# A hybrid encoder layer on one core: the first group's weights in another layout, and part of them on another queue

## The chip, the cores and the metric

The kernel runs on one core of a Trainium2 chip. The time is the device time of one execution in microseconds, the median of several runs. The engines are TensorE (PE, with its weight loads as PEld), VectorE (DVE), ScalarE (ACT), GpSimd (POOL) and SyncE (SP); SyncE and ScalarE both issue DMAs, each on a queue of its own.

## What is computed

A layer of 1024 positions and width 1024 in float32. One wide product, two mixers, a gated merge, an output product and a layer norm:

```
h = x @ w_in + b_in                      # 1024 x 6144: xa za xb zb ga gb
ya = RG-LRU(causal_conv4(xa)) * silu(za)
yb = MultiScalePool(xb) * silu(zb)
y  = (sigmoid(ga) * (ya @ w_proj_a) + sigmoid(gb) * (yb @ w_proj_b)) @ w_out + b_out
out = LayerNorm(alpha * x + y)
```

The change concerns the start of the first product alone: the blocks of `ga` that are computed first.

## The kernel before, in words

Every float32 matrix is split into a high part (a cast to fp32r on ScalarE, `CAST`) and a low part (raw minus high, on VectorE, `TENSOR_TENSOR`), and each product is three matmul passes: high by high, weight high by data low, weight low by data high (`passes`, lines 454 to 457). The input product is done in groups of two weight blocks of 128 columns. Later groups use sums of quarters so as to need seven products for eight; the first one is plain.

That first group takes the blocks 32 and 36 of `w_in` (block 0 and block 1 below; `first` in line 959). In DRAM a block lies as 128 partitions x 8 chunks x 128 columns. The contraction has eight chunks of 128, split in two halves (called `h` in the weights' views, `kh` elsewhere) of four chunks `k`. Tiles `w0r0`, `w0r1` take the raw blocks, `w0h` and `w0l` their high and low parts (lines 959 to 961). `dma_w0(n, a, b, h)` loads of block n the chunks a to b of the halves h (line 971), and `split_w0` makes its high and low part (line 975). A chunk of one half is a row of 128 columns, 512 B; two chunks side by side are 1 KB.

The data come as `xq`, in four chunks q with two rows each, loaded into `xr` by `dma_x` (line 978), split by `split_x` into `x13h`/`x13l` (two quarters), `xb` and `x`. A row of 1024 columns holds two quarters of 512 positions. TensorE's order for chunk 0 is fixed (lines 1082 to 1092): quarter (0, 0) with block 0, in two pieces of 256 columns; quarter (1, 1) with block 0, which needs the second half of block 0's first weights and the second half of row 0 (`dma_x(0, 0, HALF[1])`); quarters (0, 0) and (1, 1) with block 1, which need block 1's first weights (`dma_w0(1, 0, 1)`); then quarter (0, 1), which reads `xb`. Its second matmul reads the low part. Six matmuls of zeros (`ps_warm`) run before all that.

The order of the instructions is not that of the text. A planner (`Plan.order`, lines 252 to 379) runs all tasks through a modelled time and emits them in the order in which it starts them. TensorE and GpSimd keep the written order. On the others, of the tasks that are ready the one with the smallest due time goes first, then the one written first. The due time of a task is the smaller of what its readers leave it (their due time less its own modelled time) and TensorE's modelled clock where it is written plus `late`, which is 40 us, and within `nc.within(-2 * SOON)` it is -4 us (line 266). The modelled clock is 2.88 us where the first loads are written. A load on SyncE is costed at 270 GB/s and 0.07 us of issue, on ScalarE at 270 GB/s and 0.45 us. A task may be held back for one that is about to be ready and due earlier (lines 358 to 361). `sum57(q)` (line 1042) is a VectorE subtraction of 128x1024 for the sums of quarters; it needs row 0 and the first half of row 1, and is due later than the low parts around it.

The loads are written in this order: the first half of block 0's first weights (ScalarE's queue), the two pieces of row 0's first half (SyncE, within -4 us), the second half of block 0's first weights (ScalarE's), block 1's first weights (ScalarE's), row 0's second half, row 1 in two halves, and the rest on SyncE. Later loads wait for a free completion semaphore of an earlier one.

Of the kernel before, what the change touches and what calls it, by code (L numbers as in the profile page):

```python
# [11 lines left out]
F32 = mybir.dt.float32  # L12
F32R = mybir.dt.float32r
AF = mybir.ActivationFunctionType
ALU = mybir.AluOpType

P = 128
S = 1024
D = 1024
NK = D // P  # L20
# [380 lines left out]
def layer_kernel(ctx: ExitStack, tc: tile.TileContext, xq, x, w_in, par, wg, w_pool, wpa, wpb, w_out, rows, out):  # L401
    nc = Plan(tc)
# [18 lines left out]
    def wt(name, dt=F32R, shape=(P, 2, H)):  # L421
        return wpool.tile(list(shape), dt, tag="w", name=name)
# [7 lines left out]
    def et(name):  # L430
        return epool.tile([P, H], F32, tag="e", name=name)
# [9 lines left out]
    V, A = nc.vector, nc.scalar  # L441
# [8 lines left out]
    def split(raw, hi, lo):  # L450
        A.copy(hi, raw)
        V.tensor_tensor(lo, raw, hi.bitcast(F32), ALU.subtract)
# [147 lines left out]
    def blocks_of(kind, c):  # L600
        if kind == "A":
            return XA + c, ZA + c
        if kind == "B":
            return XB + c, ZB + c
        sec = GA if c < 4 else GB
        return sec + c % 4, sec + c % 4 + 4
# [297 lines left out]
    def b_pool(g):  # L904
# [15 lines left out]
        if g == 1:  # L920
# [5 lines left out]
    sp, m, nl, y, z, z2, acc = (const.tile([P, 8], F32, name=n)  # L926
                                for n in ("sp", "sp_m", "sp_nl", "sp_y", "sp_z", "sp_z2", "sp_acc"))
# [29 lines left out]
    for i in range(WARM):  # L957
        nc.tensor.matmul(psw, warm[:, 0:P], warm, start=True, stop=True)
    first = blocks_of(*order[0])
    wr, wh, wl = [[f(f"{t}{n}") for n in range(2)] for t, f in  # L960
                  (("w0r", lambda n: wt(n, F32)), ("w0h", wt), ("w0l", wt))]
# [6 lines left out]
    def w0_part(t, n, a, b):  # L968
        return t[n].rearrange("p h (k m) -> p h k m", m=P)[:, :, a:b, :]

    def dma_w0(n, a, b, h=slice(0, 2)):

        (A if a == 0 else nc.sync).dma_start(w0_part(wr, n, a, b)[:, h], w_in[first[n]].rearrange("p (h k) m -> p h k m", h=2)[:, h, a:b, :])

    def split_w0(n, a, b, h=slice(0, 2)):
        split(*(w0_part(t, n, a, b)[:, h] for t in (wr, wh, wl)))

    def dma_x(q, i, sl=slice(0, S)):
        nc.sync.dma_start(xr[q][i][:, sl], xq[q, i][:, sl])
# [21 lines left out]

    PARTS = [slice(0, H // 2), slice(H // 2, H)]
    dma_w0(0, 0, 1, slice(0, 1))
    with nc.within(-2 * SOON):
        for sl in PARTS:
            dma_x(0, 0, sl)
    dma_w0(0, 0, 1, slice(1, 2))
    dma_w0(1, 0, 1)
    dma_x(0, 0, HALF[1])
    dma_x(0, 1, HALF[0])  # L1010
    dma_x(0, 1, HALF[1])
# [65 lines left out]
    def each(f, qs, *a):  # L1077
        for q in qs:
            f(q, *a)

    split_w0(0, 0, 1, slice(0, 1))
    for kh, h in ((0, 0), (1, 1), (0, 1), (1, 0)):
        if kh == h == 1:
            split_w0(0, 0, 1, slice(1, 2))
        for sl in PARTS if kh == h == 0 else (slice(0, H),):
            split_x(0, kh, h, sl)
            mm0(0, kh, h, 0, sl)
        if kh == h == 1:
            split_w0(1, 0, 1)
            mm0(0, 0, 0, 1)  # L1090
        if kh or h:
            mm0(0, kh, h, 1)
# [264 lines left out]
    for i, (n, j) in enumerate(steps):  # L1357
# [7 lines left out]
        if j == 1:  # L1365
            a, c, m1, um = [[None] * KQ for _ in range(4)]
        X_, W_ = ([(hi_[:, k, :], lo_[:, k, :]) for hi_, lo_ in ops[i][o:o + 2] for k in range(2)] for o in (0, 2))
        for g in range(KQ):
# [17 lines left out]
            if (n, j) in DONE:  # L1386
                d, h = DONE[n, j]
                d += g
                if j == 3:
                    t, u = ps, et(f"c12_{n}{g}") if n == "b" else None  # L1390
                else:
                    t = u = m1[g] if j == 2 else um[g][:, HALF[h]]
# [12 lines left out]
            if (n, j, g) in CASTS:  # L1405
                k = CASTS.index((n, j, g))
# [89 lines left out]
    a, c = ([None] * KQ for _ in range(2))  # L1496
# [89 lines left out]
```

## Time and profile before

| | us |
|---|---|
| median of three runs (742.25 to 745.42) | 742.84 |
| the profiled execution | 743.09 |
| its span, first to last instruction | 741.3 |
| TensorE busy | 732.1 |
| VectorE busy | 599.6 |
| ScalarE busy | 459.0 |

The rows come from that one profiled execution; times count from the start of its span. A line of the timeline gives start, length, engine, line (L388 for all, since one line emits every task), operation, output<-inputs, and in brackets how long the engine sat idle before it and who ended that. Matmul lengths include their pipelined end, so the distance between starts tells the pace. Buffer numbers are left out of names, so `w0h` stands for either block.

### The profile page before, as it was taken

The numbers are of one execution on the slowest core, as the hardware profiler recorded it, in microseconds if no ns is written. First come the engines' busy times: TensorE is split into PE (matmuls) and PEld (weight loads), VectorE is DVE, ScalarE is ACT, GpSimd is POOL, SyncE is SP. The second block draws the span as 40 slices with busy tenths as digits, with TensorE's granted clock in tenths as the row PEclk, the third lists the DMA queues.
The fourth block names the chain that finished last, engine by engine and source line by source line (L and its number), as shares of the span: only waits on it lengthen the run. The fifth ranks groups of instructions, "written<-read, shape, count | busy, mean of one in ns | idle before, by whom it ended". The sixth has DMA issues, their size and how long they took to land.

```text
span 741.3 us, 8792 instructions
## 1 busy us (share of the span) xinstructions
PE 732.1 (99%) x3249; PEld 599.0 (81%) x3249; DVE 599.6 (81%) x749; ACT 459.0 (62%) x587; POOL 68.2 (9%) x118
## 2 busy tenths in 40 slices
PE   8999999999999999999999999999999999999996
PEld 6887887888788878888888888888888888888885
DVE  7999796959696878977986767879948886999676
ACT  7686959686877868688844445446543555324473
POOL 0071011111101111100011000100000000000021
PEclk9999999999999999999999999999999999999999
DMA  8237988588988989842187944998679996758657
GB/s 328 96 137 194 273 190 259 139 243 217 307 166 214 321 214 281 213 115 99 45 200 155 213 113 157 277 336 319 229 248 298 317 330 230 261 206 233 179 88 139
DMA packets 64227, 158.98 MB, mean 214 GB/s; under 512 B 4340, under 2 KB 8308, under 8 KB 64120
## 3 DMA queue, kind: packets, MB, share of 16 engines
q1 hardware_dynamic: 43512, 106.26, 41.3%
q0 software_dynamic: 20112, 51.91, 33.6%
q8 instruction: 25, 0.41, 0.2%
q10 hardware_dynamic: 560, 0.26, 0.1%
q14 instruction: 18, 0.15, 0.1%
HBM read 137.43 MB, written 77.07 MB: 289 GB/s over the span
## 4 chain that ended last, share of the span: by engine, by line
PE 98%; DMA 1%; DVE 1%; DVEq 0%; issue 0%
PE a_A L388 11%; PE a_B L388 11%; PE a_G L388 11%; PE oa L388 6%; PE pa_a L388 6%; PE pa_b L388 6%; PE c_B L388 6%; PE c_A L388 6%; PE c_G L388 5%; PE ps_pool L388 3%; PE oc L388 3%; PE pc_b L388 3%; PE pc_a L388 3%; PE e_B L388 3%; PE e_A L388 3%; PE ps_s L388 3%
## 5 line engine op out<-in xcount | busy, mean ns | idle before, releaser
L388 ACT ACT_TABLE_LOAD x38 | 48.8, 1283 | 3.0 <-issue 2.3
L388 DVE TENSOR_TENSOR i<-i,xc 128x1024 f32<-128x1024 f32 x8 | 9.8, 1224 | 26.6 <-ACT i L388 26.6
L388 DVE SCALAR_TENSOR_TENSOR xc<-xp,par_sb,xc 128x1024 f32<-128x1024 f32 x24 | 30.7, 1279 | 0.3
L388 PE MATMUL pa_a<-oh,oh 128*128 128x512 f32 x64 | 24.9, 389 | 0.0
L388 PE MATMUL pa_a<-oh,ol 128*128 128x512 f32 x64 | 24.9, 389 | 0.0
L388 PE MATMUL pa_b<-oh,oh 128*128 128x512 f32 x64 | 24.9, 389 | 0.0
L388 PE MATMUL pa_b<-ol,oh 128*128 128x512 f32 x64 | 24.9, 389 | 0.0
L388 PE MATMUL pa_b<-oh,ol 128*128 128x512 f32 x64 | 24.9, 389 | 0.0
L388 PE MATMUL pa_a<-ol,oh 128*128 128x512 f32 x64 | 24.9, 389 | 0.0
L388 ACT ACTIVATE zb<-zb,par_sb 128x1024 f32<-128x1024 f32 (+1 forms) x16 | 15.0, 939 | 13.7 <-DVE zb L388 13.6
L388 ACT ACTIVATE r<-ps_g,par_sb 64x512 f32<-64x512 f32 x32 | 21.9, 684 | 2.1 <-PE ps_g L388 1.2
L388 ACT ACTIVATE i<-ps_g,par_sb 64x512 f32<-64x512 f32 x32 | 21.9, 685 | 1.9 <-DVE r L388 1.4
L388 PE MATMUL c_A<-x64h,wd_A 128*128 128x512 f32 x64 | 21.0, 389 | 0.0
L388 PE MATMUL c_B<-x64h,wd_B 128*128 128x512 f32 x64 | 21.0, 389 | 0.0
L388 PE MATMUL ps_pool<-mixh,wp 128*128 128x512 f32 x64 | 20.6, 393 | 0.0
L388 POOL DMA_DIRECT2D out<-y x7 | 8.5, 1210 | 132.1 <-ACT sd L388 118.7
L388 PE MATMUL e_A<-x,wah_A 128*128 128x512 f32 x64 | 19.7, 389 | 0.0
L388 PE MATMUL e_B<-x,wah_B 128*128 128x512 f32 x64 | 19.7, 389 | 0.0
L388 POOL COPY paced<-pace 128x1 f32<-128x1 f32 x17 | 6.6, 387 | 128.7 <-ACT pace L388 128.7
L388 PE MATMUL c_G<-x64h,wd_G 128*128 128x512 f32 x56 | 18.4, 389 | 0.0
L388 DVE TENSOR_TENSOR_SCAN r<-a,i 128x1024 f32<-128x1024 f32 x8 | 18.3, 2282 | 0.1
L388 PE MATMUL e_G<-x,wah_G 128*128 128x512 f32 x56 | 17.2, 389 | 0.0
(521 smaller groups left out, 2535.9 us busy)
## 6 DMA issues: line engine op xcount, KB each, us to landing
sg<-sg SPq DMA_DIRECT2D x16, 512.0 KB, 3.6
ra_A<-in_w_in SPq DMA_DIRECT2D x8, 512.0 KB, 7.2
rb_A<-in_w_in SPq DMA_DIRECT2D x8, 512.0 KB, 7.8
xb<-bias SPq DMA_DIRECT2D x4, 1024.0 KB, 15.9
ya<-r SPq DMA_DIRECT2D x8, 512.0 KB, 6.3
xb<-in_x POOLq DMA_DIRECT2D x4, 1024.0 KB, 9.3
ra_B<-in_w_in SPq DMA_DIRECT2D x8, 512.0 KB, 4.8
rb_B<-in_w_in SPq DMA_DIRECT2D x8, 512.0 KB, 6.2
```

The source lines that it names most:

```text
L388: getattr(getattr(nc, t.op[0]), t.op[1])(*a, **k)
```

## The change

Block 0 and block 1 are stored in DRAM chunk by chunk with the two halves side by side (chunk k of half 0, chunk k of half 1), the same on the chip in the raw tile. A load of one chunk with both halves is then one row of 1 KB for each partition, where it was two of 512 B, and one of two chunks is a row of 2 KB, where it was two of 1 KB. The split reads the raw tile through a view that puts the halves back in place. ScalarE's queue is used for chunk 0 of block 0 only; block 1's first weights go on SyncE's queue. The second half of block 0's first weights and block 1's first weights are now written within the block of the small due times. The high part of block 0's first half is made by VectorE (`V.tensor_copy`) where ScalarE made it.

```diff
+    def w0_raw(n, a, b):
+        t = wr[n].rearrange("p a b -> p (a b)").rearrange("p (k h m) -> p h k m", h=2, m=P)
+        return t[:, :, a:b, :]
+
     def dma_w0(n, a, b, h=slice(0, 2)):
 
-        (A if a == 0 else nc.sync).dma_start(w0_part(wr, n, a, b)[:, h], w_in[first[n]].rearrange("p (h k) m -> p h k m", h=2)[:, h, a:b, :])
-
-    def split_w0(n, a, b, h=slice(0, 2)):
-        split(*(w0_part(t, n, a, b)[:, h] for t in (wr, wh, wl)))
+        lo_, hi_ = 2 * P * a + P * h.start, 2 * P * (b - 1) + P * h.stop
+        (A if n == a == 0 else nc.sync).dma_start(wr[n].rearrange("p a b -> p (a b)")[:, lo_:hi_],
+                                                  w_in[first[n]].rearrange("p k m -> p (k m)")[:, lo_:hi_])
+
+    def split_w0(n, a, b, h=slice(0, 2), high=A.copy):
+        raw, u, v = w0_raw(n, a, b)[:, h], w0_part(wh, n, a, b)[:, h], w0_part(wl, n, a, b)[:, h]
+        high(u, raw)
+        V.tensor_tensor(v, raw, u.bitcast(F32), ALU.subtract)
...
     with nc.within(-2 * SOON):
         for sl in PARTS:
             dma_x(0, 0, sl)
-    dma_w0(0, 0, 1, slice(1, 2))
-    dma_w0(1, 0, 1)
+        dma_w0(0, 0, 1, slice(1, 2))
+        dma_w0(1, 0, 1)
...
-    split_w0(0, 0, 1, slice(0, 1))
+    split_w0(0, 0, 1, slice(0, 1), V.tensor_copy)
...
+    w0 = blocks(w_in[0])
+    for n in (32, 36):
+        w0[n] = w0[n].reshape(P, 2, 4, P).transpose(0, 2, 1, 3).reshape(P, NK, P)
...
-        "w_in": blocks(w_in[0]),
+        "w_in": w0,
```

## Rows read from the trace of the kernel before

**Rows 1.** The page, busy time of each engine (us, share of span, instructions).
```profile
PE 732.1 (99%) x3249; PEld 599.0 (81%) x3249; DVE 599.6 (81%) x749; ACT 459.0 (62%) x587; POOL 68.2 (9%) x118
```

**Rows 2.** Waits of TensorE from 10 us on: total, times, longest.
```profile
PE ps_s L388 <- DVE xb L388: 0.3, 1, 0.3
```

**Rows 3.** Chain that ended last, in order of time: start, length, what.
```profile
0.72 3.21 DMA w0r<-in_w_in
...
29.08 2.72 PE a_A L388 x12
```

**Rows 4.** Timeline of TensorE, 4 to 14 us.
```profile
4.42 0.58 PE L388 MATMUL ps_s<-x13h,w0h 128*128 128x256 f32 x1
...
5.49 0.41 PE L388 MATMUL ps_s<-x13l,w0h 128*128 128x256 f32 x1
5.71 0.41 PE L388 MATMUL ps_s<-x13h,w0l 128*128 128x256 f32 x1
...
6.47 0.79 PE L388 MATMUL ps_s<-x13l,w0h 128*128 128x512 f32 x1
...
7.75 0.50 PE L388 MATMUL ps_s<-x13h,w0h 128*128 128x512 f32 x1
...
9.27 0.39 PE L388 MATMUL ps_s<-xb,w0h 128*128 128x512 f32 x1
9.95 0.50 PE L388 MATMUL ps_s<-xb,w0h 128*128 128x512 f32 x1 [0.30 <-DVE xb L388]
10.29 0.40 PE L388 MATMUL ps_s<-xb,w0l 128*128 128x512 f32 x1
```

**Rows 5.** Timeline of ScalarE, 0 to 12 us.
```profile
3.77 0.41 ACT L388 CAST x13h<-xr 128x256 fp32r<-128x256 f32 x1 [0.17 <-DMA xr<-in_xq]
...
4.61 0.29 ACT L388 CAST w0h<-w0r 128x128 fp32r<-128x128 f32 x1
5.08 0.62 ACT L388 CAST x13h<-xr 128x512 fp32r<-128x512 f32 x1 [0.17 <-DMA xr<-in_xq]
7.30 0.40 ACT L388 CAST w0h<-w0r 128x256 fp32r<-128x256 f32 x1 [1.60 <-DMA w0r<-in_w_in]
```

**Rows 6.** Timeline of VectorE, 0 to 14 us.
```profile
4.21 0.43 DVE L388 TENSOR_TENSOR x13l<-xr,x13h 128x256 fp32r<-128x256 f32 x1 [2.80 <-ACT x13h L388]
4.55 0.28 DVE L388 TENSOR_TENSOR w0l<-w0r,w0h 128x128 fp32r<-128x128 f32 x1
4.75 0.42 DVE L388 TENSOR_TENSOR x13l<-xr,x13h 128x256 fp32r<-128x256 f32 x1
...
5.73 0.69 DVE L388 TENSOR_TENSOR x13l<-xr,x13h 128x512 fp32r<-128x512 f32 x1 [0.36 <-ACT x13h L388]
7.74 0.42 DVE L388 TENSOR_TENSOR w0l<-w0r,w0h 128x256 fp32r<-128x256 f32 x1 [1.31 <-ACT w0h L388]
8.08 1.22 DVE L388 TENSOR_TENSOR t<-xr,xr 128x1024 f32<-128x1024 f32 x1
9.21 0.69 DVE L388 TENSOR_TENSOR xb<-xr,xb 128x512 fp32r<-128x512 f32 x1
```

**Rows 7.** DMAs issued at 1.64, 1.66 and 2.12: count, KB, us to landing.
```profile
xr<-in_xq SPq DMA_DIRECT2D x1, 256.0 KB, 3.4
w0r<-in_w_in ACTq DMA_DIRECT2D x1, 128.0 KB, 5.6
...
xr<-in_xq SPq DMA_DIRECT2D x1, 256.0 KB, 4.6
```

**Rows 8.** Stretches: busy us by engine, granted clock, DMA share, GB/s.
```profile
7.30:8.30 1.00, 0.91 (x3) 0.39 (x3) 0.56 (x2) 1.00 (x3) 0.00 (x0) 1.00 0.98 308
11.10:12.30 1.20, 1.20 (x7) 0.99 (x6) 1.20 (x5) 1.20 (x3) 0.00 (x0) 1.00 1.03 365
...
12.00:28.00 16.00, 16.00 (x72) 13.24 (x71) 16.00 (x21) 12.17 (x17) 0.00 (x0) 1.00 0.64 251
```

**Rows 9.** Waits of the weight loads from 32 us on, one of four.
```profile
PEld ps_g L388 <- ACT wah_G L388: 0.4, 1, 0.4
```

## The prediction

> **What bounds the kernel now.** I read four views, in this order: the page's busy line, the waits of TensorE after the first 10 us, the chain of waits, and the start engine by engine. The busy line gives TensorE 732.1 us [rows 1]. From 10 us to the end it has one wait left, of 0.3 us on a low part `xb` [rows 2], and that is the one that ends at 9.95. So from 10 us on TensorE is the bound without a gap, and whatever its stream gains or loses before that is carried to the end one for one. The chain says the same: a transfer of `w0r` to 3.93 at its head, and from 29.08 on twelve matmuls in 2.72 us, 0.227 us each [rows 3]. The change can act only in the first 10 us.
>
> There TensorE's matmuls read like this [rows 4]. The first real one starts at 4.42. Two 256-column ones are 0.22 us apart (5.49, 5.71), which is the lower of the clock's levels, 1.2 GHz; the later 0.227 us for 512 columns is the upper, 2.4 GHz. The granted clock reads 1.00 for every stretch of the start [rows 8], so here the spacing tells the level; it changes at about 7.5 us, in a stretch in which TensorE was nearly always busy. Between 6.47 and 10.29 stand three things:
> - block 1's first matmul starts at 7.75. ScalarE waited 1.60 us for its weights, to cast them at 7.30 [rows 5].
> - from 9.27 to 9.95 TensorE waits for the low part of `xb`: 0.68 us where 0.23 would do. VectorE began that low part only at 9.21, because at 8.08 it had started `sum57` (128x1024, written as t), and that began so late because the low part of block 1's weights stood before it and waited 1.31 us [rows 5, 6].
> - the matmul at 9.95 takes 0.34 to the next one, 0.11 too much.
>
> All three hang on one transfer: ScalarE's third DMA, 128 KB, took 5.6 us from its issue at about 1.66, so it landed near 7.3 [rows 7].
>
> **The change, part by part.**
>
> *Block 1's first weights on SyncE's queue, third in it.* In the written order the block gets the due time of the x parts before it (2.88 - 4 = -1.12); the second half of chunk 0's row (called xH1 here, 256 KB) has -0.53 by its reader. So SP issues the two x parts, then these weights, then xH1. What a third SP transfer does is shown: xH1 was issued at 1.64 and landed 3.4 us later, at 5.05; the fourth took 4.6 from 2.12, so 6.70 [rows 7]. Half the bytes in the same place should land no later than 5.05, against 7.3 now.
>
> What it costs: xH1 becomes fourth. Its landing is bounded by 5.05 (no delay) and 6.70 (the old fourth place). I take 5.05 plus the time of 128 KB at 365 GB/s, 0.36: 5.41. That is nearer the lower end, since the fourth place at 6.70 had 256 KB ahead of it instead of 128 and the slow ScalarE transfer beside it.
>
> *Order on ScalarE and VectorE.* By the planner's own due times the cast of block 1's weights now precedes that of xH1, and its low part precedes xH1's on VectorE; before, both stood behind. So a new wait stands ahead of xH1. It costs nothing while the weights land before xH1.
>
> From rows: xH1's cast starts 0.03 after landing (5.08 for 5.05), its low part 0.65 later (5.73), the matmul that reads it 0.74 after that (6.47) [rows 4 to 6]. From 5.41: 5.44, 6.09, 6.83. The third matmul of that quarter starts 0.43 later, at 7.26, still at the lower level, and block 1's first at about 7.59, with the level changing at 7.5 as before. Its weights are long there. Seven more at 0.227 bring the second `xb` matmul to 9.18, if its low part is there. That low part: `sum57` starts when VectorE has done xH1's low part and the first half of row 1 has landed (about 6.7 to 6.8, since as many bytes have passed by then); 6.79, then 1.13 to the low part (8.08 to 9.21) and 0.74 to the matmul (9.21 to 9.95): 8.66. That is before 9.18, with 0.5 us to spare. So 9.95 becomes 9.18, a gain of 0.77, and the slow restart goes too, 0.11: **0.88 us**.
>
> The bounds: xH1 at 5.05 gives the second `xb` matmul at about 9.0, a gain of 1.06. xH1 at 6.70 puts its low part at 7.38, its matmul at 8.12, block 1 at 8.57 and the second `xb` matmul at 10.16: a loss of 0.10.
>
> *The halves of block 0's first quarter.* Both stay on ScalarE's queue, but the second now has the due time -1.12 and the first, outside the block, about -0.15 by its reader: the planner issues the second half first. So the half that TensorE needs first is now second. The first one issued landed at 3.93 [rows 3]; the second one had landed when its cast began at 4.61 [rows 5]. VectorE takes its high part now, as a copy of 128x128; no row shows a VectorE copy, and the nearest are its 128x128 subtraction, 0.28 us and 0.20 to the next start (4.55, 4.75), and the cast of the same size on ScalarE, 0.29 [rows 5, 6]. Queued behind the copy on VectorE are the low parts of the x pieces, and TensorE waits for these. The worst case: copy at 4.61, then 0.20, 0.34, 0.20, 0.34, 0.20 and 0.34 for the copy and the five low parts ahead of xH1's, which then starts at 6.23 instead of 6.09: 0.14 us lost. At a landing of 4.45 it is nothing. I take nothing; TensorE starts some 0.3 us later, which xH1 hides.
>
> *ScalarE loses one DMA issue* before its table load; it already waits 0.17 us for x before the first cast at 3.77 [rows 5], so this gains nothing.
>
> *Rows of 1 and 2 KB.* Five transfers get rows twice as long: block 1's first, two second quarters (512 B to 1 KB each), two last halves (1 KB to 2 KB). With 512 B rows the queue moved 308 GB/s, with 1 KB rows 365 [rows 8]: 128 KB take 0.43 and 0.36, so some 0.07 for each, about 0.35 us of transfers. TensorE waits for none of these transfers after 10 us, so this pays nothing beyond the first, which is in the sum. It covers a TensorE that runs 0.9 us ahead, though. The raw tile is now read in pieces of 128 columns: the old form had such pieces too (a 128x256 cast of weights 0.40, the contiguous x piece 0.41), so nothing [rows 5]. The new layout is made on the host.
>
> *Behind it.* VectorE is full from 12 to 28 us, 16.00 of 16.00 [rows 8], so TensorE's gain must be VectorE's too. `sum57` starts 1.3 us earlier (8.08 to 6.79), which is more than 0.88.
>
> The sum: 743.09 profiled (span 741.3 and 1.8 around it) less 0.88 is 742.2. The profiled run lies 0.25 above the median 742.84, so I forecast **742.0**.
>
> **Rivals.**
> - *No net gain.* xH1 takes the old fourth place's landing, 6.70, or the half that comes second costs its 0.14 as well: 0.1 to 0.2 lost, 742.9 to 743.1. For it: the first microseconds move less than the later ones. Against it: fewer bytes are ahead.
> - *Slower: the weights are late at the head of two queues.* If block 1's weights still land at 7.3, ScalarE casts them at 7.30 and xH1 at 7.61, xH1's low part starts at 8.26, its matmul at 9.00, block 1 at 9.45, the second `xb` matmul at 11.04: 1.0 lost, 743.8. It decides from a landing after about 6.3. Against it: two transfers issued within 0.02 us of each other, 256 KB on SP in 3.4 us and 128 KB on ScalarE's queue in 5.6 [rows 7]; so the queue matters. The Trainium skill (DMA: Bandwidth & Descriptors, section Issuing engines are not separate DMA queues) says that the issuing engine saves only issue time, since all run on the same 16 DMA engines; by that rule alone the weights would land as late as before. The rows just named disagree with that reading of it.
> - *Slower: the plan is redrawn.* The planner orders all engines from modelled times. Its SP transfers move by 128 KB at its 270 GB/s, 0.49 us, as a block, so few pairs should swap; but a swap can put a wait into TensorE's stream. The nearest row is a gate weight load that ScalarE's `wah` held up by 0.4 [rows 9]; with eight gate steps that is 3.2, less the 0.88: 745.2. It decides from new waits of over 0.9 in all.
> - *The clock rises later*, since TensorE pauses longer before its first real matmul. If it came later by as long as from 4.42 to 7.5, 3.1 us, these would hold 7.2 matmuls at 0.43 that take 1.6 at 0.227: 1.5 lost, 743.5 with the gain.
>
> **How the numbers follow.** Forecast (a gain of 0.5 to 1.1) 0.58; no net gain 0.17; late weights 0.06; a redrawn plan 0.12; a later clock 0.05; a larger gain, from a redrawn plan, 0.02. What this kernel's measurement can tell from no change is 0.5%, 3.7 us. All of the start's loss that this change reaches is 1.1 us, so faster by more needs something else: 0.02. Slower by more needs a third or so of the redrawn plans: 0.04. The rest, 0.94, lies within. The range goes from 741.1 (the full 1.06, and the spread of some tenths between runs) to 744.1 (late weights and a late clock with it); the redrawn plan's far end is left out.
>
> **What would show it.** SP's third transfer is the 128 KB of `w0r`, landing by 5.1; the cast of 128x256 weights stands before xH1's and waits little; block 1's first matmul at about 7.6; the wait on `xb` gone and 512-column matmuls 0.23 apart through 9.2; the chain's first piece of group A0 at 28.2 instead of 29.08; no new TensorE wait later. Wrong would be: xH1 landing after 6.3; a TensorE wait behind 10 us; a low part of `xb` later than 9.2; a clock that changes after 9 us.

## The result

The changed kernel is slower: 744.49 us median (22 runs, 742.77 to 745.92) against 742.86 (22 runs, 742.24 to 745.42), a ratio of 1.0020 (95% interval 1.0014 to 1.0026). The forecast was 742.0, and the range ended at 744.1. Of the 22 times, 6 lie from 742.77 to 743.42 and 16 from 743.91 to 745.92; of the kernel before, 21 lie from 742.24 to 743.54 and one at 745.42. So the change has not moved all runs by the same amount; it has moved most of them into an upper group.

The profiled execution took 744.30 (span 742.5). TensorE's timeline, to lay beside [rows 4] (start, length, operation, idle before and who ended it):

```profile
4.71 0.55 PE L388 MATMUL ps_s<-x13h,w0h 128*128 128x256 f32 x1 [0.34 <-ACT x13h L388]
5.06 0.47 PE L388 MATMUL ps_s<-x13l,w0h 128*128 128x256 f32 x1
5.49 0.58 PE L388 MATMUL ps_s<-x13h,w0l 128*128 128x256 f32 x1
5.87 0.41 PE L388 MATMUL ps_s<-x13h,w0h 128*128 128x256 f32 x1
...
6.29 0.41 PE L388 MATMUL ps_s<-x13h,w0l 128*128 128x256 f32 x1
7.20 0.79 PE L388 MATMUL ps_s<-x13h,w0h 128*128 128x512 f32 x1 [0.49 <-ACT x13h L388]
7.93 0.79 PE L388 MATMUL ps_s<-x13l,w0h 128*128 128x512 f32 x1
...
9.80 0.63 PE L388 MATMUL ps_s<-x13h,w0l 128*128 128x512 f32 x1
10.23 0.54 PE L388 MATMUL ps_s<-x13h,w0h 128*128 128x512 f32 x1
10.61 0.39 PE L388 MATMUL ps_s<-x13l,w0h 128*128 128x512 f32 x1
...
11.53 0.39 PE L388 MATMUL ps_s<-xb,w0l 128*128 128x512 f32 x1
...
12.22 0.39 PE L388 MATMUL ps_s<-xb,w0l 128*128 128x512 f32 x1
```

Three more lines of the kernel before:

```profile
8.09 0.40 PE L388 MATMUL ps_s<-x13l,w0h 128*128 128x512 f32 x1
8.33 0.40 PE L388 MATMUL ps_s<-x13h,w0l 128*128 128x512 f32 x1
...
10.99 0.39 PE L388 MATMUL ps_s<-xb,w0l 128*128 128x512 f32 x1
```

Three things differ. The first real matmul starts at 4.71 (4.42 before), and the three behind it come 0.35, 0.43 and 0.38 apart where back-to-back 256-column ones at the lower level are 0.21 apart. Quarter (1,1) starts at 7.20, after a pause from 6.50, and its second matmul at 7.93 (6.47 before). And from there the 512-column matmuls stay 0.43 apart, the lower level of 1.2 GHz, until 10.23; before, the spacing of 0.23 was there from 8.09. The wait on `xb` of [rows 2] is gone, as forecast. The last line of each is block 1's third `xb` matmul. In the kernel before it started at 10.99, 1.23 earlier; the two profiled times differ by 744.30 - 743.09 = 1.21. So the whole difference is made in the first 12 us. What is left of the profiled time behind this matmul is 732.07 to 732.11 in all five profiles of the two kernels (e12, e13 and e14 below are the other three).

Where the data came from, beside [rows 7] (issues of SP at 2.11 and 1.64: KB, us to landing):

```profile
xr<-in_xq SPq DMA_DIRECT2D x1, 256.0 KB, 4.4
w0r<-in_w_in SPq DMA_DIRECT2D x1, 128.0 KB, 4.2
```

Block 1's first weights, now SP's third transfer, landed at 5.8 (7.3 before), and xH1, now its fourth, at 6.5 (5.05 before). ScalarE's timeline, beside [rows 5] (same columns as TensorE's):

```profile
5.83 0.40 ACT L388 CAST w0h<-w0r 128x256 fp32r<-128x256 f32 x1 [1.06 <-DMA w0r<-in_w_in]
6.53 0.62 ACT L388 CAST x13h<-xr 128x512 fp32r<-128x512 f32 x1 [0.30 <-DMA xr<-in_xq]
```

VectorE's, beside [rows 6]:

```profile
4.34 0.23 DVE L388 CAST w0h<-w0r 128x128 fp32r<-128x128 f32 x1 [2.94 <-DMA w0r<-in_w_in]
4.48 0.75 DVE L388 TENSOR_TENSOR x13l<-xr,x13h 128x256 fp32r<-128x256 f32 x2
5.15 0.48 DVE L388 TENSOR_TENSOR w0l<-w0r,w0h 128x128 fp32r<-128x128 f32 x2
```

VectorE's copy of block 0's first half waits at the head of its queue to 4.34; then come the low parts of both x pieces, and only then the low parts of block 0's weights, the first of which TensorE's third matmul needs.

### The profile page after: what moved, and what is told of

The parts are those of the page before. It is cut to its first block, busy times and chain, and to the rows that moved or that the text cites. A ratio compares the mean times of both kernels' runs of the same rounds, so it can differ in the third digit from the quotient of the medians.

```text
span 742.5 us, 8793 instructions
## 1 busy us (share of the span) xinstructions
PE 732.9 (99%) x3249; PEld 600.1 (81%) x3249; DVE 600.0 (81%) x750; ACT 459.5 (62%) x586; POOL 67.7 (9%) x118
## 4 chain that ended last, share of the span: by engine, by line
PE 98%; DMA 1%; DVE 0%; SPq 0%; DVEq 0%; ACT 0%; issue 0%
PE a_A L388 11%; PE a_B L388 11%; PE a_G L388 10%; PE oa L388 6%; PE pa_a L388 6%; PE pa_b L388 6%; PE c_B L388 6%; PE c_A L388 6%; PE c_G L388 5%; PE ps_s L388 3%; PE oc L388 3%; PE ps_pool L388 3%; PE pc_b L388 3%; PE pc_a L388 3%; PE e_B L388 3%; PE e_A L388 3%
```

## The experiments

Each was timed beside the kernel before on the same chip (742.84, 742.72, 742.77 and 742.67 in the four groups of runs). Ratios are to those runs; they are not the quotients of the two medians. In all, 7 of the 126 runs of the kernel before lie at 743.9 or above, so it has the upper group too, but rarely. The changed kernel itself was timed again only singly (e13, e14), so its 744.49 stands beside these medians from a group of its own.

| run | median us (range, runs) | ratio, 95% interval |
|---|---|---|
| e1 xH1 third again | 747.43 (746.73 to 747.47, 5) | 1.0059, 1.0046 to 1.0073 |
| e2 order alone | 742.80 (742.60 to 743.87, 11) | 1.0002, 0.9994 to 1.0011 |
| e3 layout alone | 742.41 (742.15 to 744.02, 11) | 1.0001, 0.9992 to 1.0009 |
| e4 second pause filled | 743.45 (742.31 to 744.00, 11) | 1.0007, 0.9998 to 1.0016 |
| e5 first half first | 743.80 (742.64 to 744.43, 11) | 1.0011, 1.0003 to 1.0020 |
| e6 first pause filled | 742.94 (742.68 to 744.92, 11) | 1.0008, 0.9999 to 1.0017 |
| e7 before, five zeros | 743.13 (742.30 to 743.78, 11) | 1.0006, 0.9997 to 1.0015 |
| e8 no VectorE copy | 743.40 (742.67 to 745.48, 11) | 1.0012, 1.0003 to 1.0021 |
| e9 both pauses filled | 742.55 (742.33 to 742.97, 11) | 0.9998, 0.9989 to 1.0006 |
| e10 no layout | 743.75 (742.66 to 745.99, 12) | 1.0012, 1.0003 to 1.0020 |
| e11 layout and zeros | 742.29 (742.17 to 744.19, 11) | 1.0000, 0.9992 to 1.0009 |
| e15 candidate | 742.49 (742.23 to 744.50, 11) | 1.0000, 0.9991 to 1.0009 |

The zeros are matmuls of the tile `warm`, as in the kernel's own start; they leave the sums alone. The expectations name theories by letters. P: the loss comes from xH1's place, fourth instead of third. L: it comes from the new layout of the rows. H: it comes from the longer pause ahead of the first real matmul. C: it comes from the clock, whose rise is put off by pauses in TensorE's stream. S or V: it comes from VectorE's copy and the slow start behind it.

**First question: the place in the queue, or the layout.**

e1, the changed kernel with block 1's first weights outside the block of small due times:

```diff
         dma_w0(0, 0, 1, slice(1, 2))
-        dma_w0(1, 0, 1)
+    dma_w0(1, 0, 1)
```

> The changed kernel with one part undone: block 1's first weights are written outside the block of small due times again, so that SP issues xH1 (the second half of row 0) third and these weights fourth. Theory P (place): the change loses because xH1 went from third to fourth place and landed at 6.51 instead of 5.05, so that TensorE pauses from 6.51 to 7.20 before quarter (1,1). Then here xH1 lands at 5.0 to 5.4, that pause is gone, the clock changes near 7.5 and not at 10.5, and the time is 742.0 to 742.9. Theory L (layout): the rows of 1 KB are slow to start, whatever their place; then xH1 is still late or block 1's weights land after 7.3, and the time stays above 743.8.

xH1 had landed by 4.87, when its cast began, and the pause before quarter (1,1) was gone, as theory P had it; the time was 747.43 all the same. The waits of TensorE (total us, times, longest) tell why:

```profile
PE c_G L388 <- ACT wbh_G L388: 1.0, 1, 1.0
PE c_G L388 <- DVE wbl_G L388: 0.6, 1, 0.6
```

```profile
54.69 0.63 PE L388 MATMUL c_G<-x57h,wbh_G 128*128 128x512 f32 x1
55.12 0.63 PE L388 MATMUL c_G<-x57l,wbh_G 128*128 128x512 f32 x1
```

Both waits stand at 51 to 54 us. Moving one load had changed the planner's order far behind the start (on SP, ScalarE and VectorE some hundred places), and TensorE then met a group's weights that were not ready; after the two pauses the clock fell: from 54.3 to 57.7 the granted clock is 0.50 and matmuls stand 0.43 apart, as in the two lines of TensorE's timeline. So this run says nothing of xH1's place by its time; it is what the rival of a redrawn plan looks like. At the start the spacing still was 0.43 up to 9.6, without any pause before quarter (1,1), so theory P's change of the clock near 7.5 was missed as well.

e2, the kernel before with the order alone:

```diff
-        (A if a == 0 else nc.sync).dma_start(...
+        (A if n == a == 0 else nc.sync).dma_start(...
...
-    dma_w0(0, 0, 1, slice(1, 2))
-    dma_w0(1, 0, 1)
+        dma_w0(0, 0, 1, slice(1, 2))
+        dma_w0(1, 0, 1)
```

> The kernel before with the queue and the due times of the change alone (block 1's first weights on SP, third; second half of block 0's first weights first on ScalarE's queue); old layout, old rows of 512 B and 1 KB, high part on ScalarE. Theory P: as slow as the changed kernel, 743.9 to 745.0, with xH1 landing at 6.4 or later and the clock often late. Theory L: as the kernel before, 742.4 to 743.2.

742.80: theory P missed. e3, the layout alone (the changed kernel with queue, due times and ScalarE's cast as before):

```diff
-        (A if n == a == 0 else nc.sync).dma_start(...
+        (A if a == 0 else nc.sync).dma_start(...
...
-        dma_w0(0, 0, 1, slice(1, 2))
-        dma_w0(1, 0, 1)
+    dma_w0(0, 0, 1, slice(1, 2))
+    dma_w0(1, 0, 1)
...
-    split_w0(0, 0, 1, slice(0, 1), V.tensor_copy)
+    split_w0(0, 0, 1, slice(0, 1))
```

> The changed kernel's layout alone, with the queue, the due times and the engine of the high part of the kernel before. Theory P: as the kernel before or a little better, 742.3 to 743.0, block 1's first weights landing a little before 7.3 on ScalarE's queue. Theory L: as the changed kernel, 743.9 to 745.

742.41, with seven times from 742.15 to 742.70 and four from 743.47 to 744.02. By the ratios the layout alone doesn't lose, and neither does the order alone. But the layout alone already moved the landings (issues at 1.64 and 1.65: KB, us to landing):

```profile
xr<-in_xq SPq DMA_DIRECT2D x1, 256.0 KB, 4.1
w0r<-in_w_in ACTq DMA_DIRECT2D x1, 128.0 KB, 4.4
```

Block 1's weights, still on ScalarE's queue, landed at 6.08, where theory P had a little before 7.3; xH1, still third on SP's, landed at 5.76 (5.05 before). e10 is the change without the layout, which is e2 with VectorE's copy (`split_w0` takes the engine as in the change):

```diff
...
-    split_w0(0, 0, 1, slice(0, 1))
+    split_w0(0, 0, 1, slice(0, 1), V.tensor_copy)
```

> The change without the layout: queue, due times and VectorE's copy of block 0's first half in the old layout with its rows of 512 B and 1 KB. Theory S (serial start): order and copy together make the loss, whatever the rows; 743.6 to 744.8. Rival L2 (the rows count): block 1's first weights and xH1 come earlier in the old rows, as in the run with the order alone (4.93 and 5.55); then 742.6 to 743.2.

743.75, as theory S had it: with the copy, the order loses in the old layout too. The landings of rival L2 didn't come back: in e10's profile the old rows brought block 1's weights at 5.83 and xH1 at 6.47, as late as the new ones. The other way round, e8 is the changed kernel with that high part on ScalarE:

```diff
-    split_w0(0, 0, 1, slice(0, 1), V.tensor_copy)
+    split_w0(0, 0, 1, slice(0, 1))
```

> The changed kernel with the high part of block 0's first half on ScalarE again, nothing else. The half still comes second and lands near 4.3; ScalarE casts it by 4.6 and the first real matmul starts at about 4.65. Theory H: as the changed kernel, 744.0 to 744.9. Rival V (VectorE's copy at the head of its queue is to blame): 742.5 to 743.1, as with the order alone in the old layout.

743.40, between the two expectations: better than the changed kernel's 744.49, worse than e2. How the copy acts is seen in TensorE's first matmuls (its timeline in each). e2:

```profile
4.31 0.44 PE L388 MATMUL ps_s<-x13h,w0h 128*128 128x256 f32 x1
4.59 0.28 PE L388 MATMUL ps_s<-x13l,w0h 128*128 128x256 f32 x1
4.71 0.31 PE L388 MATMUL ps_s<-x13h,w0l 128*128 128x256 f32 x1
4.86 0.28 PE L388 MATMUL ps_s<-x13h,w0h 128*128 128x256 f32 x1
```

e10:

```profile
4.38 0.55 PE L388 MATMUL ps_s<-x13h,w0h 128*128 128x256 f32 x1
4.73 0.47 PE L388 MATMUL ps_s<-x13l,w0h 128*128 128x256 f32 x1
5.16 0.57 PE L388 MATMUL ps_s<-x13h,w0l 128*128 128x256 f32 x1
5.53 0.31 PE L388 MATMUL ps_s<-x13h,w0h 128*128 128x256 f32 x1
```

Both start alike. Then e2 needs 0.55 to the fourth matmul and e10 1.15, because the low parts queue behind the copy, and in that order. But more than the copy differs between these two profiles. e2 is at the upper level there already (0.12 from 4.59 to 4.71, against 0.21 at the lower one), which for three matmuls makes up to 0.27 of the 0.60; and with the same loads, block 1's weights and xH1 landed at 4.93 and 5.55 in e2, 0.9 earlier than in e10. So the copy's own share of the loss isn't shown. e5 moves the first half back to the front of ScalarE's queue in the changed kernel:

```diff
-    dma_w0(0, 0, 1, slice(0, 1))
     with nc.within(-2 * SOON):
+        dma_w0(0, 0, 1, slice(0, 1))
```

> The changed kernel with one line moved: the first half of block 0's first weights is written inside the block of small due times too, so that ScalarE issues it first again and the second half after it. All other orders stay. Theory H (head): the loss comes from the pause between the matmuls of zeros (the last starts at 3.75 and takes 0.43, to 4.17) and the first real one (4.71 instead of 4.42), in which the half that TensorE needs was second in its queue; a longer pause leaves the clock low until 9 to 10.5 us. Then here this half lands near 3.8, the first real matmul starts at 4.2 to 4.35, the clock changes by 7.6, and the time is 742.0 to 743.1, with a spread like that of the kernel before. Rival P (xH1's later landing decides): TensorE still pauses before quarter (1,1), and the time stays at 744.1 to 744.8.

743.80, five times from 742.64 to 742.84 and six from 743.80 to 744.43. The first real matmul did start earlier, at 4.17, and the profiled run (742.77) was at the upper level by 5.9; but the median lies in neither theory's range. The third matmul came 0.76 behind the second (4.52, 5.28), and quarter (1,1) waited as in the changed kernel. No single part of the order was found to make the loss.

**Second question: the later data, or the clock.** The two groups of times ask for a cause that differs from run to run. e4 puts zeros into the pause before quarter (1,1):

```diff
             split_w0(0, 0, 1, slice(1, 2))
+            for i in range(2):
+                nc.tensor.matmul(psw, warm[:, 0:P], warm, start=True, stop=True)
```

> The changed kernel with two matmuls of zeros (512 columns, 0.43 us each at the lower level) written for TensorE between quarter (0,0) and quarter (1,1), where it pauses from 6.51 to 7.20. Nothing else of its start moves. Theory C (clock): most of the loss is that TensorE's pause leaves the clock low until 10.5 us; then with the pause filled it changes near 7.5 more often and the time falls by 0.7 to 1.5, to 743.0 to 743.8, though quarter (1,1) starts up to 0.2 later. Rival (delay alone): only the later landing counts; then 744.4 to 744.8.

743.45, within theory C's range, and none above 744.00. One thing more changed, in e9 and e15 too: from the first matmul of group A0 (tile a_A, at 28 to 32 us) to the last of all, the profiles of these three have 704.46 us and the changed kernel's 704.81, the difference spread over the whole stretch. So these three are some 0.35 faster by something that is not the start's; with that put back e4's median is 743.80, the upper end of theory C's range. The planner had put a few tasks of ScalarE and VectorE there into another order; but that order is the one of the kernel before, which has 704.77, so it isn't the cause, and the cause stays open. e6 puts one into the pause ahead of the first real matmul, where the instructions are emitted:

```diff
                 getattr(getattr(nc, t.op[0]), t.op[1])(*a, **k)
+                if t.eng == "PE" and t.args[0].tile.name == "ps_warm":
+                    warm = getattr(self, "warm", 0) + 1
+                    self.warm = warm
+                    if warm == WARM:
+                        nc.tensor.matmul(*a, **k)
```

> The changed kernel with one more matmul of zeros behind the six, put in where the instructions are emitted, so that no other order moves. It takes TensorE from 4.17 to 4.60, ahead of the first real matmul at 4.71; no data come earlier. Theory H: the clock changes by 7.6 instead of 10.5 in most runs, and the time falls by 0.8 to 1.8, to 742.7 to 743.7. Rival (the later data alone count, and when the clock changes is chance): 744.2 to 744.8.

742.94, as theory H had it, yet with three times from 743.98 to 744.92. All orders here are those of the changed kernel, and xH1 landed at 6.28, within its 6.16 to 6.93 in the three profiles of that kernel. e7 takes one zero from the kernel before:

```diff
+                if t.eng == "PE" and t.args[0].tile.name == "ps_warm":
+                    self.warm = getattr(self, "warm", 0) + 1
+                    if self.warm == WARM:
+                        continue
                 getattr(getattr(nc, t.op[0]), t.op[1])(*a, **k)
```

> The kernel before with the last of the six matmuls of zeros left out where the instructions are emitted; no other order moves, and no data come later. The pause ahead of the first real matmul grows from 0.25 (4.17 to 4.42) to 0.68 (3.74 to 4.42). Theory H: the clock changes after 9 us in most runs, the time rises by 0.8 to 2, to 743.6 to 744.8, and spreads over 2 us or more. Rival: as before, 742.6 to 743.0.

743.13, below theory H's range and a little above the rival's: a pause of 0.7 at the head alone costs 0.4 by the medians, which is not clear of the noise (the interval reaches down to 0.9997). So the head's pause is not the whole cause either. e9 has both fillings, the edits of e4 and e6 together:

> The changed kernel with zeros in both of TensorE's pauses: one more matmul of zeros ahead of the first real one, and two ahead of quarter (1,1). No data come earlier, and quarter (1,1) may start up to 0.2 later. Theory C (clock): the whole loss is that TensorE's pauses between 4.2 and 7.2 let the clock rise later in most runs; with both filled, hardly any run is above 743.7, and the median is 742.5 to 743.1. Rival (data): the later data cost something by themselves that the zeros can't give back; then 743.4 to 744.5, as with either pause filled alone or worse.

742.55, and all eleven times from 742.33 to 742.97. Its data come hardly earlier than in the changed kernel (TensorE's timeline of e9):

```profile
4.17 0.63 PE L392 MATMUL ps_warm<-warm 128*128 128x512 f32 x1
4.67 0.56 PE L388 MATMUL ps_s<-x13h,w0h 128*128 128x256 f32 x1
...
6.11 0.63 PE L388 MATMUL ps_warm<-warm 128*128 128x512 f32 x2
7.14 0.49 PE L388 MATMUL ps_s<-x13h,w0h 128*128 128x512 f32 x1 [0.41 <-ACT x13h L388]
7.87 0.50 PE L388 MATMUL ps_s<-x13l,w0h 128*128 128x512 f32 x1 [0.23 <-DVE x13l L388]
8.21 0.39 PE L388 MATMUL ps_s<-x13h,w0l 128*128 128x512 f32 x1
8.44 0.40 PE L388 MATMUL ps_s<-x13h,w0h 128*128 128x512 f32 x1
```

Quarter (1,1) starts at 7.14 and its second matmul at 7.87, where the profile of the changed kernel has 7.20 and 7.93; but the spacing is already 0.23 (8.21, 8.44). With three matmuls of zeros, which compute nothing, the upper group is gone and the median is 1.94 us lower, 0.35 of which is not the start's. The two medians are from different groups of runs, in which the kernel before had 742.86 and 742.77.

Two more profiles of the changed kernel pair a time with the level:

> The changed kernel once more, for a second profile beside a second time. Theory C: the time and the moment at which the clock rises go together: a run of 744.5 or more shows the rise after 9 us, one below 743.2 before 7. Rival: the landings of the loads differ instead, by as much as the time.

> The changed kernel a third time, for a third pair of a time and a rise of the clock. Theory C and the rival as for the second profile: 744.5 or more with a rise after 9 us, below 743.2 with one before 7.

They took 742.78 and 746.14. Neither has an edit. TensorE's timeline of e13 (742.78):

```profile
5.69 0.28 PE L388 MATMUL ps_s<-x13h,w0h 128*128 128x256 f32 x1
5.81 0.28 PE L388 MATMUL ps_s<-x13l,w0h 128*128 128x256 f32 x1
...
7.58 0.50 PE L388 MATMUL ps_s<-x13l,w0h 128*128 128x512 f32 x1 [0.23 <-DVE x13l L388]
...
10.68 0.39 PE L388 MATMUL ps_s<-xb,w0l 128*128 128x512 f32 x1
```

and of e14 (746.14):

```profile
5.85 0.41 PE L388 MATMUL ps_s<-x13h,w0h 128*128 128x256 f32 x1
6.06 0.42 PE L388 MATMUL ps_s<-x13l,w0h 128*128 128x256 f32 x1
...
8.35 0.80 PE L388 MATMUL ps_s<-x13l,w0h 128*128 128x512 f32 x1
...
12.78 0.63 PE L388 MATMUL ps_s<-xb,w0l 128*128 128x512 f32 x1
13.21 0.99 PE L388 MATMUL ps_s<-xb,w0h 128*128 128x512 f32 x2
14.04 0.40 PE L388 MATMUL ps_s<-xb,w0l 128*128 128x512 f32 x1
```

In the first, 256 columns take 0.12 from 5.69 on, the upper level; in the second, 512 columns take 0.43 up to 13.21. The same instructions, the same orders. The difference of 3.36 us at block 1's third `xb` matmul (10.68, 14.04) splits into 0.77 by data (the second matmul of quarter (1,1), 7.58 and 8.35; xH1 landed at 6.2 and 6.9) and 2.59 by the level (3.10 and 5.69 us from there on). The rival has a quarter of it, theory C the rest. Since nothing was edited between them, the moment of the rise varies by itself; filling the pauses makes the upper group rarer (16 of 22 times in the changed kernel, 3 of 11 in e6, none in e9).

**A third: the wait that the forecast counted on.**

> The kernel before once more, for a second profile of it. If its landings are the same in every run, block 1's first weights land at 7.2 to 7.3 again and TensorE waits 0.4 to 0.7 for the low part of xb. If they differ from run to run (the run with five matmuls of zeros, same loads, had them at 6.72 and no such wait), this profile may be without that wait, and then it was no part of the kernel's usual time.

This is the kernel before, with no edit: 742.90, and TensorE again waited for the low part of `xb`:

```profile
9.07 0.39 PE L388 MATMUL ps_s<-xb,w0h 128*128 128x512 f32 x1
9.79 0.50 PE L388 MATMUL ps_s<-xb,w0h 128*128 128x512 f32 x1 [0.33 <-DVE xb L388]
```

Block 1's first weights landed at 7.1. So the wait is in both profiles of the kernel before ([rows 4] and this one). It is missing in e7's, which has the same loads, but where block 1's weights landed at 6.7 instead of 7.3; a wait that hangs on a landing can come and go by itself.

**Candidates.** e11 is e3 with a zero of 128 columns ahead of the first real matmul and one of 512 ahead of quarter (1,1):

```diff
                 getattr(getattr(nc, t.op[0]), t.op[1])(*a, **k)
+                if t.eng == "PE" and t.args[0].tile.name == "ps_warm":
+                    self.warm = getattr(self, "warm", 0) + 1
+                    self.zero = a
+                    if self.warm == WARM:
+                        nc.tensor.matmul(a[0][:, 0:P], a[1], a[2][:, 0:P], **k)
+                if t.eng == "PE" and t.args[0].tile.name == "ps_s0_0":
+                    self.first = getattr(self, "first", 0) + 1
+                    if self.first == 6:
+                        nc.tensor.matmul(*self.zero, start=True, stop=True)
```

> A candidate: the layout alone (old queue, old due times, high part on ScalarE) with a matmul of zeros of 128 columns ahead of the first real one and one of 512 ahead of quarter (1,1). The layout alone had two groups of times, 742.2 to 742.7 and 743.5 to 744.0. Theory C: the upper group belongs to runs in which the clock rises late; the zeros take most of it away: median 742.2 to 742.7, at most one run above 743.4. Rival: the groups come from the data; nothing changes, 742.3 to 742.9 with three or four runs above 743.4.

The lowest median of all, 742.29, as theory C had it, but two times at 744.2 instead of one at most; its profile (743.27) has the upper level by 5 us and a wait of 0.6 on the low part of `xb`, since the first half of row 1 landed at 8.1 there. So not every slow time is the clock's. e15 is e9 with the high part on ScalarE and the first half first:

```diff
-    dma_w0(0, 0, 1, slice(0, 1))
     with nc.within(-2 * SOON):
+        dma_w0(0, 0, 1, slice(0, 1))
...
-    split_w0(0, 0, 1, slice(0, 1), V.tensor_copy)
+    split_w0(0, 0, 1, slice(0, 1))
```

> A candidate: the changed kernel with both pauses filled by zeros, the high part of block 0's first half on ScalarE and that half first in its queue. Theory C: with the clock out of the way and the start no later than before, 742.2 to 742.6 and no run above 743.3. Rival: xH1's landing in fourth place (6.1 to 6.5) sets the start, the order of the halves gives nothing, and the time is that of the kernel with both pauses filled, 742.4 to 742.7.

742.49, which both theories allow, and one time of eleven at 744.5; no better than e9. No version was shown to beat the kernel before: e9, e11 and e15 all have intervals across 1.

## Why the prediction was wrong

- *What bounds the kernel, and that only the first 10 us matter:* right. The difference of the profiled times is there at 12 us, and e9 shows no wait after it. The wait on `xb` went, and block 1's weights came 1.5 earlier.
- *The landing of xH1, the term that was mis-sized.* It was bounded by 5.05 and 6.70 and taken at 5.41. It landed at 6.51 in the profiled run, and at 6.08 to 6.93 in all runs with this order and layout, close to the end that gave a loss of 0.10. Under it lay a bound that fell: a transfer of half the bytes in third place should land by 5.05; it landed at 5.38 to 6.25. Bytes ahead of a transfer do not fix its landing in these first microseconds. From there on the later rate held: xH1 landed 0.62 to 0.71 behind the weights in every run with this order, and 256 KB at the 365 GB/s of [rows 8] are 0.72. Why the weights came so late stays open. The sum had no term for the layout, which moved xH1 by itself: third on SP's queue it landed at 5.01 to 5.10 in the two profiles of the kernel before and in e7's, and at 5.76 and 5.81 in e3 and e11, where the weights on ScalarE's queue came earlier instead. Yet the rows alone don't decide: in e1, with the weights behind it, xH1 had landed by 4.87, and as third transfer the weights with old rows landed at both 4.93 and 5.83 (e2, e10).
- *Thus the gain of 0.88 was about nothing*, with the clock out of the way. The steps behind the landing held: 6.51 and the working's 1.42 give 7.93, where the second matmul of quarter (1,1) started. Between its own bounds a landing at 6.51 puts the second `xb` matmul at 9.97, a gain of 0.09. The times say the same: 742.78 (e13), and 742.9 for e9 with the 0.35 put back, against medians of 742.7 to 742.9. The case of no net gain was the right one for the data; it had 0.17.
- *The order on VectorE failed.* The working put the copy, then an x low part, then a weight low part, and so on, 0.14 at worst, hidden by xH1. Both x low parts came before the first weight low part. That spread TensorE's first matmuls over 1.16 us instead of 0.86 (4.71 to 5.87; 4.42 to 5.28 before). The data hid that, as the working had it: quarter (0,0) was done at 6.50, and quarter (1,1) waited for xH1 to 7.20. The medians of e10 and e2 are 0.95 apart, far above the copy's own 0.23, but their landings and their level differ too, so what the copy costs stays open.
- *The clock failed most.* The working kept its change at 7.5 and gave a later one 0.05 and a price of 1.5. The third `xb` matmul was due at 9.41 (9.18 and 0.23) and came at 11.53 in the profiled run: 0.79 of these 2.12 is the landing's, which by the bounds makes it 10.20, and 1.33 the level's. In the changed kernel it came at 10.4, before 5.7, and at about 14, and cost up to 2.6; 16 of 22 times are in the upper group. What the prediction said of it was half right: it named the longer pause ahead of the first matmul, but not the pauses after it, and it treated one profile's moment as the kernel's. Two of its signs of being wrong came true: xH1 after 6.3 and a clock that changes after 9.
- *Rivals.* The late weights at the head of two queues didn't happen (5.8 is before 6.3). The redrawn plan didn't happen to this change but to e1, with 1.6 of waits and a fall of the clock. The weights did land earlier, at 5.8 against 7.3, but that the queue did it isn't shown, since the rows changed too. With the new rows they landed at 6.08 and 5.98 on ScalarE's queue (e3, e11) and at 5.38 to 6.25 on SP's; with the old ones at 6.72 to 7.28 on ScalarE's and at 4.93 and 5.83 on SP's. The Trainium skill (DMA: Bandwidth & Descriptors, section Issuing engines are not separate DMA queues) says that the issuing engine saves only issue time. Read as in the prediction, the queue then changes nothing: the runs agree for the new rows and disagree for the old. And what the weights gained, xH1 lost (6.5 against 5.05).
- *A reading.* The two stretches of [rows 8] were taken for rows of 512 B and of 1 KB. Their rows are mixed, 0.72 and 1.15 KB on average (0.31 MB in 429 packets, 0.44 MB in 383); the sum doesn't hang on the difference.

## What to carry to other kernels

A start that waits for data has two clocks: the data's and TensorE's. Cost an edit there by the pauses it leaves in TensorE's stream as well as by what lands when, take the level's change from several profiles and not from one, and try a few matmuls of zeros in the pauses before moving loads. Where a planner orders the whole program, compare its orders after every edit: in e1 one load of the changed kernel was moved, and its profile is 4.0 us longer behind the start, most of it at 51 to 58 us.

## What the runs showed of the hardware

The level rose at very different moments in runs of one program. In three executions of the changed kernel the first three real matmuls start within 0.1 us of each other (4.71, 5.06, 5.49; 4.68, 4.97, 5.46; 4.69, 5.04, 5.47), and 2.4 GHz is there before 5.7 in the second, from 10.4 in the first and near 14 in the third. The Trainium skill (TensorE: Matmul & The Clock Gate, section Part 1: The HAM clock gate (the "warmup" mystery)) says that the point of the change varies from run to run of one kernel; these rows agree, and with the pauses filled (e9) its effect on the time was not seen in eleven runs.

With rows of 512 B, ScalarE's third transfer (128 KB) landed at 6.72 to 7.28 and SP's third (256 KB, issued within 0.03 us of it) at 5.01 to 5.10; with rows of 1 KB in ScalarE's it was 5.98 and 6.08, and SP's, whose rows hadn't changed, landed at 5.81 and 5.76. A VectorE copy of 128x128 from float32 to fp32r took 0.23 us, against 0.29 on ScalarE.
